# Gated levels on quarters of the array, four level slots, and the output gate moved to the output stage

## The chip, the cores and the metric

One core of a Trainium2 chip runs the kernel. A core has five engines that run their own instruction queues in order: TensorE (PE, matrix products; its weight loads are listed as PEld), VectorE (DVE), ScalarE (ACT), GpSimd (POOL) and SyncE (SP, which here issues all DMA transfers). They wait for each other by semaphores. Operands lie in SBUF, which has 128 partitions; matrix products end in PSUM. The metric is the device time of one execution in microseconds.

## What is computed

One layer for 2048 latent tokens of 1024 channels, with 256 context tokens ahead of them: normalisation and modulation, a projection to the inputs of two mixers, gated linear attention (GLA) and the gated delta rule (GDN), each run over the tokens in both directions with 4 heads, and an output part that normalises, gates and mixes both. What the change touches is the attention inside a chunk of GLA and the gates of the output:

```
def gla_chunked(q, k, v, g, s0):
...
        diff = bi[:, :, :, None, :] - bi[:, :, None, :, :]
        dec = jnp.exp(jnp.where(causal[:, :, None], diff, -jnp.inf))
        att = jnp.einsum('bhtd,bhsd,bhtsd->bhts', qi, ki, dec)
        o = jnp.einsum('bhtd,bhde->bhte', qi * jnp.exp(bi), s) + jnp.einsum('bhts,bhse->bhte', att, vi)
...
    ya = rmsnorm(oa, gla_onorm).reshape(b, t, GLA_V) * jax.nn.silu(ag)
    yb = rmsnorm(ob, gdn_onorm).reshape(b, t, GDN_V) * jax.nn.silu(bg)
    merged = gates[..., :D_MODEL] * jnp.matmul(ya, w_gla_out) + gates[..., D_MODEL:] * jnp.matmul(yb, w_gdn_out)
    return jnp.matmul(merged, w_o)
```

The decay in `att` is one number per pair of tokens and channel, so `att` isn't one matrix product of q and k. The kernel builds it from levels.

## The kernel before

The program has three stages: projections and the preparation of GDN (to about 1367 us of the profile), the recurrences (`phase_mix`, to about 1785 us), and the output (`phase_out`). A planner of the framework puts each engine's instructions in an order by its own costs, from generators that `weave` interleaves; the order on each engine is fixed when the program is built.

`phase_mix` takes 17 steps `si`. Step `si` works on two chunks of 128 tokens at once, chunk 2 + si forwards and the mirrored one backwards, for GLA in `gla_step` and, one step behind, for GDN in two `gdn_scan`. From step 8 on both directions of a chunk are there, and each step gets four `finish` generators, two for GLA (mi = 0, tile `og`) and two for GDN (mi = 1, tile `oi`).

**Levels.** `att` of the forward chunk (tile `at`, 128 keys by 128 queries by 4 heads, both directions in one tile since one fills the upper and one the lower triangle) is built for the levels m = 64, 32, 16, 8, 4, 2: at level m the pairs of tokens in the same block of 2m but different halves. For each level `gla_group` makes decayed keys `E` (L1117 on PE sums the logs of the decays, L1205 and L1208 on ACT take exponentials, L1215 on POOL multiplies by k) and decayed queries `ql` (L1214 on DVE), two levels to a group; `gla_lev` multiplies them (L1250) into one of two slots of the PSUM tile `lv` and copies what belongs to the level into `at`: for m = 64 two plain copies of a corner each on ACT (L1258), for the others a copy on DVE under a mask of all 128 columns (L1261). The levels 64 and 32 follow the step's outputs (`gla_out`, L1332 and L1337: attention times v, and q times the state `Sa`), the levels 16 and 8 and then 4 and 2 come alone later. What is next to each other in time is added by `gla_near` (L1238, L1240), and POOL starts `at` with the diagonal (L1268).

**GDN.** L1047 and L1058 multiply the state `Sb` with keys and queries, L1050, L1069, L1071 (`vn`), L1079, L1083 and L1089 go on to the new state and the output.

**Outputs.** `finish` loads the gate into a tile `fg` (4 buffers, L1388), sums the squares of the output (L1392 on ACT, four for each tile), scales it (L1395, POOL), transposes it (L1399, PE), multiplies it by gain and gate (L1400, DVE, in place in `fg`) and stores it to `d_y` (L1402). There are 32 of them, A to D in the prediction being the four of one step, in the order og, oi, oi, og. In the output stage `out_y` loads two halves of `d_y` of a block of 256 tokens (L1553, into the ring `wr` of 4 buffers) and splits each into a high and a low part (L131 on ACT, L134 on POOL), which `out_merge` (L1578) multiplies with the weights of both mixers; L1647 is the product with `w_o`. The blocks follow each other as 3, 4, 2, 5, 1, 6, 0, 7.

All transfers go out on SP in order, on 8 semaphores in turn, so that at most 8 are under way.

Of the kernel before, what the change touches and what calls it, by code (L numbers as in the profile page):

```python
# [22 lines left out]
P = 128  # L23
# [61 lines left out]
def const_i32():  # L85
    s = np.arange(P)[:, None]
    out = np.zeros((P, 2, len(MASK_LEVELS), 64), np.int32)
    for d in range(2):
        for i, m in enumerate(MASK_LEVELS):
            t = later_cols(d, m)[None, :]  # L90
            out[:, d, i, :] = ((s // (2 * m)) == (t // (2 * m))) & ((s // m) != (t // m))
    t = s.T
    pairs = [((s // (2 * m)) == (t // (2 * m))) & ((s // m) != (t // m)) for m in LEVELS[1:]]
    return np.concatenate([out.reshape(P, -1), *[x.astype(np.int32) for x in pairs]], 1)


class Build:
# [1044 lines left out]

    def slot(self):
        self.nslot += 1
        return self.lv[:, :, self.nslot % 2]

    @staticmethod
    def byhalf(ap):
# [40 lines left out]
                self.gla_kt(x[0])  # L1189

    def gla_group(self, r, i0):
        nc, q, k, at = self.nc, r["q"], r["k"], r["at"]
        E = self.gE.tile([P, 2, 2, 2, P], F32, name="E", bufs=3)
        ql = self.gq.tile([P, 2, 2, P], F32, name="ql", bufs=3)
        cols = (2 * P + i0 * P, 4 * P + i0 * P)
        for ct in range(2):
            ps = self.pe()
            v = ps.rearrange("p (l b n) -> p l b n", l=2, b=4)
            self.gla_sums(v[:, :, 1:3], r, 0, ct, cols)
            self.gla_sums(v[:, :, 0:4:3], r, 1, ct, cols)  # L1200
            for li in range(2):
                m = LEVELS[i0 + li]
                s = ps[:, 256 * li:256 * li + 256]
                if m == 64:
                    nc.scalar.activation(E[:, ct, li].rearrange("p x t -> p (x t)"), s, AF.Exp, scale=1.0 / 16)  # L1205
                    continue
                for x in range(2):
                    nc.scalar.activation(E[:, ct, li, x].rearrange("p (j e i) -> p e j i", e=2, i=m),  # L1208
                                         s[:, x * P:(x + 1) * P].rearrange("p (e j i) -> p e j i", e=2, i=m),
                                         AF.Exp, scale=1.0 / 16)  # L1210
            if ct == 0:
                yield
        for li in range(2):
            nc.vector.tensor_tensor(ql[:, li], E[:, :, li, 0], q, op=ALU.mult)  # L1214
            nc.gpsimd.tensor_tensor(E[:, :, li, 1], E[:, :, li, 1], k, op=ALU.mult)  # L1215
        yield
        return [(at, [E[:, ct, li, 1] for ct in range(2)], ql[:, li], LEVELS[i0 + li]) for li in range(2)]

    def gla_ones(self, r):
        nc, k, q = self.nc, r["k"], r["q"]  # L1220
# [11 lines left out]
        return w  # L1232

    def gla_near(self, r):
        nc, at, w = self.nc, r["at"], r["near"]
        pd = self.pe()
        for ct in range(2):
            nc.tensor.matmul(pd[:, 2 * ct:2 * ct + 2], w[:, ct], self.bones, start=True, stop=True)  # L1238
        B = [P, 4, P]
        nc.vector.copy_predicated(at, self.am[:, len(LEVELS) - 2].unsqueeze(1).broadcast_to(B),  # L1240
                                  pd[:, 0:4].unsqueeze(2).broadcast_to(B))

    def gla_lev(self, levs, behind=None):
        nc, got = self.nc, []
        for at, ks, ql, m in levs:
            ps = self.slot()
            for ct in range(2):
                for hp in range(2):
                    rows = slice(64 * hp, 64 * hp + 64)
                    mm = nc.tensor.matmul(ps[:, hp, ct], ks[ct][rows], ql[rows, ct], start=True, stop=True)  # L1250
                    self.behind(mm, behind)
                    self.last_lev = mm
            got.append((self.byhalf(at), ps, m))
        for at, ps, m in got:
            if m == 64:
                for x in range(2):
                    rows, cols = slice(64 * x, 64 * x + 64), slice(64 - 64 * x, 128 - 64 * x)
                    nc.scalar.copy(at[rows, :, :, cols], ps[rows, :, :, cols])  # L1258
            else:
                i = LEVELS.index(m) - 1  # L1260
                nc.vector.copy_predicated(at, self.am[:, i].unsqueeze(1).unsqueeze(1).broadcast_to([P, 2, 2, P]), ps)  # L1261

    def gla_step(self, f, b, prev):
        nc = self.nc
        self.gla_split(f)
        self.gla_split(b)
        at = f["at"] = f["kp"].tile([P, 4, P], F32, name="at", bufs=1)
        nc.gpsimd.tensor_tensor(at, self.diag[:, f["c"] - NCTX, :].unsqueeze(2).broadcast_to([P, 4, P]),  # L1268
                                self.ident.unsqueeze(1).broadcast_to([P, 4, P]), op=ALU.mult)
        yield  # L1270
        self.gla_ends(f)
        yield
# [10 lines left out]
        yield  # L1283
        if prev is not None:
            out, done = self.gla_out(prev, S)
        self.gla_lev(levs, out if prev is not None else None)
        if prev is not None:
            done()
            yield
            yield from self.gla_put(prev)  # L1290
        yield
        last = yield from self.gla_group(f, 4)
        yield
        self.gla_lev(more)
        yield
        self.gla_kt(b)
        f["near"] = self.gla_ones(f)
# [29 lines left out]
    def gla_out(self, pair, S):  # L1327
# [4 lines left out]
            nc.tensor.matmul(po[h % 2][:, 0, h // 2], f["at"][:, h], f["v"][:, h * P:(h + 1) * P],  # L1332
                             start=h < 2, stop=False, skip_group_check=True)
        for d, r in enumerate(pair):
            for h in range(4):
                ct, rows = h // 2, slice(64 * (h % 2), 64 * (h % 2) + 64)
                mm = nc.tensor.matmul(po[h % 2][:, d, ct], r["qe"][rows, ct], S[d][rows, ct], start=False,  # L1337
                                      stop=d == 1 and h >= 2, skip_group_check=True)

        def done():  # L1340
            o = self.og = f["prev"] if f["prev"] is not None else self.op.tile([P, 2, 4, P], F32, name="og")
# [41 lines left out]
    def finish(self, mi, l, src):  # L1383
        nc, wk = self.nc, self.wk
        if "o" in self.dbg:
            nc.sync.dma_start(self.dbg["o"][mi, l], self.flat(src))
        y = wk.tile([P, 4, P], F32, name="fg", bufs=4)
        nc.sync.dma_start(y, self.d_gate[l // 2, :, 4 * mi:4 * mi + 4, (l % 2) * P:(l % 2) * P + P])  # L1388
        sq = wk.tile([P, P], BF16, name="fsq", bufs=1)
        ss = wk.tile([P, 4], F32, name="fss", bufs=4)  # L1390
        for h in range(4):
# [5 lines left out]
        pt = self.pe()  # L1397
        for h in range(4):
            self.behind(nc.tensor.transpose(pt[:, h * P:(h + 1) * P], src[:, h], self.ident), mm)  # L1399
        nc.vector.scalar_tensor_tensor(self.flat(y), pt, self.pc[:, 64 + mi:65 + mi], self.flat(y),  # L1400
                                       op0=ALU.mult, op1=ALU.mult)
# [20 lines left out]
    def phase_mix(self):  # L1422
# [17 lines left out]
        self.am = mp.tile([P, len(LEVELS) - 1, P], I32, name="am")  # L1440
# [5 lines left out]
        self.lv = self.pool("ppg", 1, PSUM, ctx=gctx).tile([P, 2, 2, 2, P], F32, name="lv")  # L1446
# [109 lines left out]
    def out_y(self, b):  # L1556
# [2 lines left out]
        yl = yp.tile([P, 8, 256], F32R, name="yl")  # L1559
        for hf in range(2):  # L1560
            ks = slice(4 * hf, 4 * hf + 4)
            self.split(yh[:, ks], yl[:, ks], self.yraw.pop(0) if self.yraw else self.y_raw(b, hf))
        self.y2 = (yh, yl)

    def out_merge(self, b):
# [128 lines left out]
```

## Time and profile before

| | us |
|---|---|
| median of 3 runs | 2175.05 (2174.11 to 2176.63) |
| the profiled execution | 2176.2 |
| its span on the core | 2174.4 |
| PE busy in the span | 2089.3 (96%) |
| DVE, ACT, POOL busy | 1237.0, 888.1, 867.7 |

The span reaches from the first to the last instruction that the profiler saw; the execution's time has 1.8 us around it. The mean granted clock of TensorE was 0.988 of its full speed. A busy time is the union of an engine's instructions, and those of PE overlap: the time of a run of matmuls is better read from one start to the next. In a timeline, instructions of one kind that follow each other are one row with their count.

### The profile page before, as it was taken

Reading aid. Unit: us, or ns where it says so; the run is one execution under the profiler, and the core shown is the slowest. Engines: PE = TensorE matmul, PEld = TensorE weight load, DVE = VectorE, ACT = ScalarE, POOL = GpSimd, SP = SyncE. Lnnn points to the kernel's source line nnn. Section 1 sums busy time; section 2 is a strip of 40 time slices with the busy share of each in tenths; the row PEclk is TensorE's granted clock in tenths of the full one; section 3 lists DMA queues with packets and bytes.
Section 4 is the critical chain, followed back from the end, with each engine's and each line's share of the span. In section 5 each row is a group of like instructions: output and inputs, shape, how many; then the busy total and the mean of one; then the engine's idle time right before and its main releaser. Section 6 shows DMA issues by size and latency. Waiting matters only on the chain.

```text
span 2174.4 us, 39781 instructions
## 1 busy us (share of the span) xinstructions
PE 2089.3 (96%) x15072; PEld 1753.6 (81%) x15072; DVE 1237.0 (57%) x2183; ACT 888.1 (41%) x2180; POOL 867.7 (40%) x779
## 2 busy tenths in 40 slices
PE   5999999999999999999999999899989988999998
PEld 2688888888888888777777777788888887999888
DVE  3813555556777554555555555566678876344333
ACT  3644255554552223343444443344455554112111
POOL 2410122222231015665666662556566655222331
PEclk9999999999999999999999999999999989999999
DMA  7323122222222224344444443878779958443322
GB/s 279 110 85 115 50 68 64 67 62 66 61 65 81 74 84 138 118 146 146 141 147 151 129 139 114 300 279 307 262 262 312 299 177 265 131 127 116 102 85 81
DMA packets 275004, 315.67 MB, mean 145 GB/s; under 512 B 22280, under 2 KB 206716, under 8 KB 274812
## 3 DMA queue, kind: packets, MB, share of 16 engines
q1 hardware_dynamic: 274812, 313.12, 44.5%
q8 instruction: 119, 1.95, 0.4%
q14 instruction: 73, 0.60, 0.1%
HBM read 203.20 MB, written 109.84 MB: 144 GB/s over the span
## 4 chain that ended last, share of the span: by engine, by line
PE 83%; DVE 5%; ACT 4%; DMA 4%; issue 2%; SPq 1%; POOL 1%; DVEq 0%; POOLq 0%; ACTq 0%
PE pz L370 46%; PE pz L1647 8%; PE pm L1578 7%; PE pe L1117 2%; PE pz L1079 1%; PE pe L935 1%; PE pl L987 1%; PE pl L994 1%; PE lv L1250 1%; PE pl L995 1%; DMA g<-dg 1%; PE pz L1058 1%; DVE ql L1214 1%; PE pq L613 1%; ACT E L1208 1%
## 5 line engine op out<-in xcount | busy, mean ns | idle before, releaser
L370 PE MATMUL pz<-hi,wh 128*128 128x512 f32 (+1 forms) x1560 | 621.7, 399 | 1.6 <-DVE hi L133 1.6
L370 PE MATMUL pz<-lo,wh 128*128 128x512 f32 (+1 forms) x1560 | 600.6, 385 | 1.8 <-POOL lo L134 1.8
L370 PE MATMUL pz<-hi,wl 128*128 128x512 f32 (+1 forms) x1520 | 588.6, 387 | 0.0
L370 PEld LDWEIGHTS pz<-lo,wh 128*128 128x128 f32 x1560 | 294.8, 189 | 51.3 <-POOL lo L134 3.7
L370 PEld LDWEIGHTS pz<-hi,wh 128*128 128x128 f32 x1560 | 294.4, 189 | 48.0 <-DVE hi L133 2.5
L370 PEld LDWEIGHTS pz<-hi,wl 128*128 128x128 f32 x1520 | 286.3, 188 | 53.8 <-issue 0.4
L134 POOL TENSOR_TENSOR wl<-w,wh 128x1024 fp32r<-128x1024 f32 x44 | 108.8, 2475 | 437.3 <-ACT wh L131 311.9
L568 DVE SCALAR_TENSOR_TENSOR acc<-zpad,cw,acc 128x1024 f32<-128x1024 f32 x192 | 271.4, 1414 | 6.7
L1578 PE MATMUL pm<-yh,wab 128*128 128x256 f32 x1024 | 190.5, 287 | 0.9 <-ACT wab L131 0.9
L872 DVE CAST_PREDICATED U<-kit,pl 128x256 f16<-128x256 int32 x216 | 91.2, 431 | 139.4 <-PE pl L995 135.6
L1578 PEld LDWEIGHTS pm<-yh,wab 128*128 128x128 f32 x1024 | 163.5, 195 | 1.8 <-ACT wab L131 1.0
L1647 PE MATMUL pz<-wo,mh 128*128 128x512 f32 (+1 forms) x528 | 160.6, 387 | 0.0
L1578 PE MATMUL pm<-yl,wab 128*128 128x256 f32 x512 | 146.9, 287 | 0.2 <-POOL yl L134 0.2
L988 ACT CAST ppb<-pl 128x256 f16<-128x256 f32 x216 | 73.6, 374 | 167.6 <-PE pl L987 161.2
L1215 POOL TENSOR_TENSOR E<-E,ak 128x256 f32<-128x256 f32 x96 | 80.9, 863 | 101.8 <-ACT E L1205 51.6
L1647 PEld LDWEIGHTS pz<-wo,mh 128*128 128x128 f32 x528 | 98.2, 189 | 20.0
L134 DVE TENSOR_TENSOR sql<-sq,sqh 128x512 fp32r<-128x512 f32 (+1 forms) x36 | 28.0, 804 | 142.0 <-ACT sqh L131 141.8
L623 POOL TENSOR_TENSOR acc<-acc,sq 128x512 f32<-128x512 f32 x32 | 51.1, 1605 | 138.4 <-ACT sq L622 90.6
L1647 PE MATMUL pz<-wo,ml 128*128 128x512 f32 (+1 forms) x264 | 101.5, 385 | 0.0
L1578 PEld LDWEIGHTS pm<-yl,wab 128*128 128x128 f32 x512 | 100.2, 196 | 0.7 <-POOL yl L134 0.4
L134 POOL TENSOR_TENSOR yl<-wr,yh 128x1024 fp32r<-128x1024 f32 x16 | 40.2, 2529 | 135.7 <-ACT yh L131 135.7
L1652 DVE TENSOR_TENSOR mt<-pz,gtb 128x512 f32<-128x512 f32 (+1 forms) x33 | 22.3, 675 | 117.0 <-PE pz L1647 114.8
(297 smaller groups left out, 4182.9 us busy)
## 6 DMA issues: line engine op xcount, KB each, us to landing
dgate<-ob SPq DMA_DIRECT2D x96, 256.0 KB
gd<-dgd SPq DMA_DIRECT2D x32, 768.0 KB
w<-in_w_in SPq DMA_DIRECT2D x44, 512.0 KB
qk<-dqkv SPq DMA_DIRECT2D x32, 512.0 KB
ga<-dgate SPq DMA_DIRECT2D x64, 256.0 KB
dqkv<-acc SPq DMA_DIRECT2D x192, 64.0 KB
dgd<-tm SPq DMA_DIRECT2D x36, 256.0 KB
dgd<-n SPq DMA_DIRECT2D x36, 256.0 KB
```

Of the source, the lines that this page charges most:

```text
L134: getattr(nc, lo).tensor_tensor(dst_lo, src, dst_hi.bitcast(F32), op=ALU.subtract)
L370: nc.tensor.matmul(ps[:, 0:n], a[:, kk, :], b[:, kk, :], start=(k == 0), stop=(k == last - 1))
L568: nc.vector.scalar_tensor_tensor(acc, src, wcol, acc, op0=ALU.mult, op1=ALU.add)
L613: nc.tensor.matmul(u[4][:, 0:u[2]], self.ones, u[3][i], start=(i == 0), stop=(i == 1))
L623: nc.gpsimd.tensor_tensor(v, v, r, op=ALU.mult)
L872: self.nc.vector.copy_predicated(out, mv, data)
L988: nc.scalar.copy(ppl, pc.rearrange("p h (j i) -> p h j i", i=m))
L1117: self.nc.tensor.matmul(out, g[:, i, ct * P:(ct + 1) * P], self.wt[:, d, cols[0]:cols[1]], start=(j == 0), stop=(j == 1))
L1215: nc.gpsimd.tensor_tensor(E[:, :, li, 1], E[:, :, li, 1], k, op=ALU.mult)
L1578: nc.tensor.matmul(ps[:, half * 256:half * 256 + 256], wab[wi][:, k, j * P:(j + 1) * P], yy[:, k, :], start=(i == 0), stop=(i == 11))
L1647: nc.tensor.matmul(ps, aa[:, k, i * P:(i + 1) * P], wo[k][wi][:, cs], start=(j == 0), stop=(j == 23))
L1652: nc.vector.tensor_tensor(sq, ps, gtb[:, cs], op=ALU.mult)
```

## The change

Four things are changed.

- A level is multiplied by quarters: 64 keys by 64 queries for one head at a time (tiles of 64 rows and 64 columns of the array, L1257), only where the level has pairs: the diagonal blocks of 64 for m < 64, the other two for m = 64. Its slot in `lv` is 64 columns wide instead of 128, and there are four in the same PSUM. Masks, the copies under a mask, and the diagonal's product go by a tile `own` of the diagonal blocks; two ACT copies at the end (L1245) put it into `at`. The state's part of the output (L1337, now L1347) goes by quarters too, with 64 queries in place of 128.
- The levels 64, 32, 16 and 8 are multiplied together behind `gla_out`; only 4 and 2 stand alone.
- `finish` has no gate for 28 of 32 tiles (all but those of block 3): ACT (mi = 0, L1420) or DVE (mi = 1, L1418) multiplies by the gain on the way out of PSUM, and `fg` has two buffers.
- `out_y` loads the gates of 7 of the 8 blocks in two transfers of 512 KB and multiplies (L1589, DVE, 128 x 1024) before the split.

```diff
     def slot(self):
         self.nslot += 1
-        return self.lv[:, :, self.nslot % 2]
+        return self.lv[:, :, self.nslot % 4]
...
     def gla_near(self, r):
...
-        B = [P, 4, P]
-        nc.vector.copy_predicated(at, self.am[:, len(LEVELS) - 2].unsqueeze(1).broadcast_to(B),
+        B = [P, 4, 64]
+        nc.vector.copy_predicated(own, self.am[:, len(LEVELS) - 2].unsqueeze(1).broadcast_to(B),
                                   pd[:, 0:4].unsqueeze(2).broadcast_to(B))
+        for x in range(2):
+            half = slice(64 * x, 64 * x + 64)
+            nc.scalar.copy(at[half, :, half], own[half])
 
     def gla_lev(self, levs, behind=None):
         nc, got = self.nc, []
-        for at, ks, ql, m in levs:
+        for r, ks, ql, m in levs:
             ps = self.slot()
             for ct in range(2):
-                for hp in range(2):
-                    rows = slice(64 * hp, 64 * hp + 64)
-                    mm = nc.tensor.matmul(ps[:, hp, ct], ks[ct][rows], ql[rows, ct], start=True, stop=True)
-                    self.behind(mm, behind)
-                    self.last_lev = mm
-            got.append((self.byhalf(at), ps, m))
-        for at, ps, m in got:
+                for x in range(2):
+                    y = x if m < 64 else 1 - x
+                    keys, qs = slice(64 * x, 64 * x + 64), slice(64 * y, 64 * y + 64)
+                    for hp in range(2):
+                        rows = slice(64 * hp, 64 * hp + 64)
+                        mm = nc.tensor.matmul(ps[keys, hp, ct], ks[ct][rows, keys], ql[rows, ct, qs], start=True, stop=True)
+                        self.behind(mm, behind)
+                        self.last_lev = mm
+            got.append((r, ps, m))
+        for r, ps, m in got:
             if m == 64:
                 for x in range(2):
                     rows, cols = slice(64 * x, 64 * x + 64), slice(64 - 64 * x, 128 - 64 * x)
-                    nc.scalar.copy(at[rows, :, :, cols], ps[rows, :, :, cols])
+                    nc.scalar.copy(self.byhalf(r["at"])[rows, :, :, cols], ps[rows])
             else:
                 i = LEVELS.index(m) - 1
-                nc.vector.copy_predicated(at, self.am[:, i].unsqueeze(1).unsqueeze(1).broadcast_to([P, 2, 2, P]), ps)
+                nc.vector.copy_predicated(self.byhalf(r["own"]),
+                                          self.am[:, i].unsqueeze(1).unsqueeze(1).broadcast_to([P, 2, 2, 64]), ps)
...
-        self.gla_lev(levs, out if prev is not None else None)
+        self.gla_lev(levs + more, out if prev is not None else None)
...
         last = yield from self.gla_group(f, 4)
         yield
-        self.gla_lev(more)
-        yield
...
         for d, r in enumerate(pair):
-            for h in range(4):
-                ct, rows = h // 2, slice(64 * (h % 2), 64 * (h % 2) + 64)
-                mm = nc.tensor.matmul(po[h % 2][:, d, ct], r["qe"][rows, ct], S[d][rows, ct], start=False,
-                                      stop=d == 1 and h >= 2, skip_group_check=True)
+            for ct in range(2):
+                for x in range(2):
+                    half = slice(64 * x, 64 * x + 64)
+                    for hp in range(2):
+                        rows = slice(64 * hp, 64 * hp + 64)
+                        mm = nc.tensor.matmul(po[hp][half, d, ct], r["qe"][rows, ct, half], S[d][rows, ct], start=False,
+                                              stop=d == 1 and ct == 1, skip_group_check=True)
...
-        y = wk.tile([P, 4, P], F32, name="fg", bufs=4)
-        nc.sync.dma_start(y, self.d_gate[l // 2, :, 4 * mi:4 * mi + 4, (l % 2) * P:(l % 2) * P + P])
+        gated = l // 2 == self.blocks[0]
+        if gated:
+            y = wk.tile([P, 4, P], F32, name="fg", bufs=2)
+            nc.sync.dma_start(y, self.d_gate[l // 2, :, 4 * mi:4 * mi + 4, (l % 2) * P:(l % 2) * P + P])
...
+        else:
+            y = wk.tile([P, 4, P], F32, name="fg", bufs=2)
+            if mi:
+                nc.vector.tensor_scalar(self.flat(y), pt, gain, None, op0=ALU.mult)
+            else:
+                nc.scalar.mul(self.flat(y), pt, gain)
...
-            self.split(yh[:, ks], yl[:, ks], self.yraw.pop(0) if self.yraw else self.y_raw(b, hf))
+            y = self.yraw.pop(0) if self.yraw else self.y_raw(b, hf)
+            if b != self.blocks[0]:
+                g = self.rp.tile([P, 8, P], F32, name="wr").rearrange("p (a b) c -> p a (b c)", b=2)
+                nc.sync.dma_start(g, self.d_gate[b][:, ks])
+                nc.vector.tensor_tensor(y, y, g, op=ALU.mult)
+            self.split(yh[:, ks], yl[:, ks], y)
```

What moves is seen best at three places. The first is TensorE's queue in a step of the first half, from the state's part of the output (L1337 before, L1347 after) to the last pair of levels. Before:

```order
L1337 MATMUL pz<-Sa_15950,q_15876 128x128 x4
L1250 MATMUL lv<-ql,E 128x128 [waits Pool_49]
L1250 MATMUL lv<-ql,E 128x128 x3
L1250 MATMUL lv<-ql,E 128x128 [waits Pool_49]
L1250 MATMUL lv<-ql,E 128x128 x3
...
L1226 MATMUL pe<-kf,g_16171 128x128 [waits DMAHW7_49,PE_49,Activation_49]
L1250 MATMUL lv<-ql,E 128x128 [waits DVE_49,Pool_49]
L1250 MATMUL lv<-ql,E 128x128 x3
...
L1047 MATMUL pz<-Sb_16343,qk 128x128 x3
L1250 MATMUL lv<-ql,E 128x128 [waits DVE_49,Pool_49]
L1250 MATMUL lv<-ql,E 128x128
```

After:

```order
L1347 MATMUL pz<-Sa_16048,q_15968 64x128 x8
L1347 MATMUL pz<-Sa_16051,q_15974 64x128 x8
L1257 MATMUL lv<-ql,E 64x64 [waits Pool_49]
L1257 MATMUL lv<-ql,E 64x64 x7
L1257 MATMUL lv<-ql,E 64x64 [waits Pool_49]
L1257 MATMUL lv<-ql,E 64x64 x7
L1257 MATMUL lv<-ql,E 64x64 [waits Pool_49]
L1257 MATMUL lv<-ql,E 64x64 x3
L1257 MATMUL lv<-ql,E 64x64 [waits Activation_49]
...
L1048 MATMUL pz<-Sb_16471,qk 128x128 x3
L1257 MATMUL lv<-ql,E 64x64 [waits DVE_49,Pool_49]
L1257 MATMUL lv<-ql,E 64x64 x3
```

Before, the three pairs of levels stand at three places, the last one behind all eight L1047. After, four levels stand behind L1347, and the last pair stands behind the first four L1048 and ahead of the other four.

The second place is ScalarE's queue in a step of the second half, around the copies of level 64 (L1258 before, L1265 after). E with 2x16x4 and 2x32x2 are the exponentials of the levels 4 and 2, `fsq` the squared sums of `finish`. Before:

```order
L1137 COPY akt<-pe 128x256 [waits PE_49]
L1208 ACTIVATE E<-pe 128x2x16x4 [waits DVE_49,PE_49]
L1208 ACTIVATE E<-pe 128x2x16x4
L1208 ACTIVATE E<-pe 128x2x32x2 x2
L1392 ACTIVATE fsq,fss<-og 128x128 [waits DMAHW0_49,DVE_49,Pool_49]
L1392 ACTIVATE fsq,fss<-og 128x128 [waits DVE_49,Activation_49]
L1392 ACTIVATE fsq,fss<-og 128x128 [waits Activation_49]
L1258 COPY at<-lv 64x2x2x64 [waits PE_49]
L1258 COPY at<-lv 64x2x2x64
L1208 ACTIVATE E<-pe 128x2x16x4 [waits PE_49]
L1208 ACTIVATE E<-pe 128x2x16x4
L1208 ACTIVATE E<-pe 128x2x32x2 x2
```

After:

```order
L1138 COPY akt<-pe 128x256 [waits PE_49]
L1404 ACTIVATE fsq,fss<-og 128x128 [waits DMAHW4_49,DVE_49,Pool_49]
L1404 ACTIVATE fsq,fss<-og 128x128 [waits DVE_49,Activation_49]
L1404 ACTIVATE fsq,fss<-og 128x128 [waits Activation_49] x2
L1265 COPY at<-lv 64x2x2x64 [waits PE_49]
L1265 COPY at<-lv 64x2x2x64
L1209 ACTIVATE E<-pe 128x2x16x4 [waits PE_49]
L1209 ACTIVATE E<-pe 128x2x16x4
L1209 ACTIVATE E<-pe 128x2x32x2 x2
L1209 ACTIVATE E<-pe 128x2x16x4 [waits PE_49]
L1209 ACTIVATE E<-pe 128x2x16x4
L1209 ACTIVATE E<-pe 128x2x32x2 x2
```

Four of the eight exponentials were ahead of the squared sums and the copies; all eight are now behind them, and the squared sums ahead of the copies are four instead of three.

The third is ScalarE's queue at the exponentials of the levels 64 and 32 of the next chunk (L1205 and L1208 before, L1206 and L1209 after), where the fourth output of the step is finished. Before:

```order
L1393 ACTIVATE fss<-fss,cb 128x4 [waits Activation_49]
L1394 ACTIVATE fss<-fss 128x4 [waits Activation_49]
L1205 ACTIVATE E<-pe 128x256 [waits PE_49]
L1208 ACTIVATE E<-pe 128x2x2x32 x2
L1205 ACTIVATE E<-pe 128x256 [waits PE_49]
L1208 ACTIVATE E<-pe 128x2x2x32 x2
L131 CAST gh_19593<-g_19567 128x256 [waits DMAHW1_49,PE_49]
L1126 ACTIVATE E_18962<-pe 128x512 [waits PE_49,Pool_49]
```

After:

```order
L1405 ACTIVATE fss<-fss,cb 128x4 [waits Activation_49]
L1406 ACTIVATE fss<-fss 128x4 [waits Activation_49]
L1206 ACTIVATE E<-pe 128x256 [waits PE_49]
L1209 ACTIVATE E<-pe 128x2x2x32 x2
L1420 ACTIVATE fg<-pe,pc 128x512 [waits DMAHW2_49,DMAHW5_49,DMAHW1_49,DVE_49]
L1206 ACTIVATE E<-pe 128x256 [waits PE_49]
L1209 ACTIVATE E<-pe 128x2x2x32 x2
L1127 ACTIVATE E_19370<-pe 128x512 [waits PE_49,Pool_49]
L1209 ACTIVATE E<-pe 128x2x4x16 [waits PE_49]
```

The product with the gain, L1420, now stands between the two halves of these exponentials. It waits on three DMA semaphores; one of them is that of the store that empties its buffer.

## Rows read from the trace of the kernel before

**Rows 1.** Windows: stretch, its us, busy us and instructions of each engine, PE clock, DMA share, GB/s.

```profile
1391.00:1604.00 213.00, 197.32 (x1937) 180.25 (x1936) 144.83 (x301) 99.16 (x382) 123.37 (x144) 0.99 0.83 289
1604.00:1760.00 156.00, 142.53 (x1376) 132.06 (x1377) 129.55 (x278) 91.51 (x448) 104.41 (x118) 1.00 0.88 285
...
1828.00:2174.00 346.00, 339.10 (x2139) 307.65 (x2137) 140.33 (x229) 62.01 (x139) 95.28 (x93) 0.99 0.36 118
```

**Rows 2.** Chain that ended last, first half: start us, us, what.

```profile
1484.75 2.05 PE pz L1079 x16
...
1507.53 2.05 PE pz L1079 x16
...
1513.15 7.88 DMA do<-oi
1521.09 6.10 DMA g<-dg
...
1596.35 6.13 DMA g<-dg
```

**Rows 3.** PE timeline, first half: start us, us to the last end, instructions, count.

```profile
1490.98 1.16 PE L1337 MATMUL pz<-Sa,q 64*128 64x128 f32 x16
1491.97 1.06 PE L1250 MATMUL lv<-ql,E 64*128 64x128 f32 x16
1492.96 0.39 PE L1117 MATMUL pe<-wt,gh 128*128 128x256 f32 x1
...
1495.01 1.16 PE L1250 MATMUL lv<-ql,E 64*128 64x128 f32 x16
...
1496.48 1.73 PE L1047 MATMUL pz<-Sb,qk 128*128 128x128 f32 x14
...
1499.25 0.39 PE L1117 MATMUL pe<-wt,gh 128*128 128x256 f32 x1
```

**Rows 4.** PE timeline, two windows, 1423.02 to 1423.06 and 1423.0 to 1424.2.

```profile
1423.03 0.42 PE L645 MATMUL pz<-gw,sc 128*32 128x256 f32 x4
...
1423.03 1.50 PE L645 MATMUL pz<-gw,sc 128*32 128x256 f32 x24
```

**Rows 5.** ACT timeline, first half.

```profile
1493.90 1.48 ACT L1208 ACTIVATE E<-pe 128x128 f32<-128x128 f32 x8
```

**Rows 6.** POOL timeline, first half.

```profile
1495.10 1.67 POOL L1215 TENSOR_TENSOR E<-E,ak 128x256 f32<-128x256 f32 x2 [1.68 <-ACT E L1208]
```

**Rows 7.** PE timeline, second half; in brackets the idle time ahead and its releaser.

```profile
1645.13 1.16 PE L1250 MATMUL lv<-ql,E 64*128 64x128 f32 x16 [1.12 <-DVE at L1261]
...
1661.78 1.16 PE L1337 MATMUL pz<-Sa,q 64*128 64x128 f32 x16
...
1666.78 1.16 PE L1250 MATMUL lv<-ql,E 64*128 64x128 f32 x16 [1.19 <-DVE at L1261]
...
1671.32 1.09 PE L1313 MATMUL pz<-av,akt 128*64 128x128 f32 x16
```

**Rows 8.** ACT timeline, second half.

```profile
1653.73 0.39 ACT L1205 ACTIVATE E<-pe 128x256 f32<-128x256 f32 x1 [0.83 <-PE pe L1117]
...
1665.85 0.80 ACT L1208 ACTIVATE E<-pe 128x128 f32<-128x128 f32 x4
...
1679.25 0.39 ACT L1205 ACTIVATE E<-pe 128x256 f32<-128x256 f32 x1 [0.83 <-PE pe L1117]
```

**Rows 9.** SP timeline: DMA issues, second half.

```profile
1650.18 1.03 SPq L1402 DMA_DIRECT2D dy<-fg  x2
...
1653.83 1.56 SPq L1388 DMA_DIRECT2D fg<-dgate  x2
...
1675.53 1.03 SPq L1402 DMA_DIRECT2D dy<-fg  x2
...
1681.31 4.27 SPq L1388 DMA_DIRECT2D fg<-dgate  x4
```

**Rows 10.** Groups of instructions, output stage: busy us, mean ns, idle before and releaser.

```profile
L134 DVE TENSOR_TENSOR wo<-wr,wo 128x1024 fp32r<-128x1024 f32 x2 | 2.4, 1222 | 3.4 <-ACT wo L131 3.4
```

More of the change, by code (lines that the diff above doesn't have):

```diff
@@ L93, in const_i32 @@
     pairs = [((s // (2 * m)) == (t // (2 * m))) & ((s // m) != (t // m)) for m in LEVELS[1:]]
-    return np.concatenate([out.reshape(P, -1), *[x.astype(np.int32) for x in pairs]], 1)
+    own = [np.where(s < 64, x[:, 0:64], x[:, 64:128]) for x in pairs]
+    return np.concatenate([out.reshape(P, -1), *[x.astype(np.int32) for x in own]], 1)
 class Build:
@@ L1191, in gla_group @@
     def gla_group(self, r, i0):
[L1192 removed]
+        nc, q, k = self.nc, r["q"], r["k"]
         E = self.gE.tile([P, 2, 2, 2, P], F32, name="E", bufs=3)
@@ L1216, in gla_group @@
         yield
-        return [(at, [E[:, ct, li, 1] for ct in range(2)], ql[:, li], LEVELS[i0 + li]) for li in range(2)]
+        return [(r, [E[:, ct, li, 1] for ct in range(2)], ql[:, li], LEVELS[i0 + li]) for li in range(2)]
     def gla_ones(self, r):
@@ L1234, in gla_near @@
     def gla_near(self, r):
-        nc, at, w = self.nc, r["at"], r["near"]
+        nc, at, own, w = self.nc, r["at"], r["own"], r["near"]
         pd = self.pe()
@@ L1266, in gla_step @@
         self.gla_split(b)
-        at = f["at"] = f["kp"].tile([P, 4, P], F32, name="at", bufs=1)
-        nc.gpsimd.tensor_tensor(at, self.diag[:, f["c"] - NCTX, :].unsqueeze(2).broadcast_to([P, 4, P]),
-                                self.ident.unsqueeze(1).broadcast_to([P, 4, P]), op=ALU.mult)
+        f["at"] = f["kp"].tile([P, 4, P], F32, name="at", bufs=1)
+        own = f["own"] = f["kp"].tile([P, 4, 64], F32, name="own", bufs=1)
+        nc.gpsimd.tensor_tensor(own, self.diag[:, f["c"] - NCTX, :].unsqueeze(2).broadcast_to([P, 4, 64]),
+                                self.id64.unsqueeze(1).broadcast_to([P, 4, 64]), op=ALU.mult)
         yield
@@ L1399, in finish @@
             self.behind(nc.tensor.transpose(pt[:, h * P:(h + 1) * P], src[:, h], self.ident), mm)
-        nc.vector.scalar_tensor_tensor(self.flat(y), pt, self.pc[:, 64 + mi:65 + mi], self.flat(y),
-                                       op0=ALU.mult, op1=ALU.mult)
+        gain = self.pc[:, 64 + mi:65 + mi]
+        if gated:
+            nc.vector.scalar_tensor_tensor(self.flat(y), pt, gain, self.flat(y), op0=ALU.mult, op1=ALU.mult)
+        else:
[4 more added lines that the diff above has]
+                nc.scalar.mul(self.flat(y), pt, gain)
         nc.sync.dma_start(self.d_y[l // 2, :, mi * 4:mi * 4 + 4, (l % 2) * P:(l % 2) * P + P], y)
@@ L1439, in phase_mix @@
             nc.vector.memset(self.bones[64 * x:64 * x + 64, 1 - x:2 - x], 0.0)
-        self.am = mp.tile([P, len(LEVELS) - 1, P], I32, name="am")
+        self.am = mp.tile([P, len(LEVELS) - 1, 64], I32, name="am")
+        self.id64 = mp.tile([P, 64], F32, name="id64")
+        for x in range(2):
+            half = slice(64 * x, 64 * x + 64)
+            nc.vector.tensor_copy(self.id64[half], self.ident[half, half])
         wt = mp.tile([P, 2, WL], F32R, name="wt")
@@ L1445, in phase_mix @@
         self.ppe = self.pool("ppe", 3, PSUM, ctx=ctx)
-        self.lv = self.pool("ppg", 1, PSUM, ctx=gctx).tile([P, 2, 2, 2, P], F32, name="lv")
+        self.lv = self.pool("ppg", 1, PSUM, ctx=gctx).tile([P, 2, 4, 2, 64], F32, name="lv")
         self.nslot, self.last_lev = 0, None
```

## The prediction

> **What bounds the kernel now.** I read the table of windows first. The projections before 1391 us aren't touched by the diff. The recurrent stage falls into two halves: in steps 0 to 7 (1391 to 1604 us) TensorE is busy 197.3 of 213 us, in steps 8 to 15 (1604 to 1760 us), where outputs are finished too, 142.5 of 156; the DMA engines are busy 83% and 88% [rows 1]. The output stage is TensorE's almost alone, 339.1 of 346 us, with DMA at 36% and DVE at 140 us [rows 1]. So there is something to win only in the two halves.
>
> The chain of waits shows what a step is. From one start of L1079 to the next an undisturbed step takes 22.8 us (1484.75 to 1507.53); the next one takes 26.3, because a store of 7.88 us and a load of 6.10 us end last in it [rows 2]. A third such piece stands at 1596.35. Where a transfer ends last, faster matmuls buy nothing. So two or three of the first eight steps gain little, and I count 0.7 of what TensorE saves there.
>
> **Levels: half the columns, four quadrants.** (Line numbers are those before; only L1420 and L1589, which are new, are those after.) Before, one level is 8 matmul instructions (4 in the code, each issued as two) on half the array's rows, 128 columns wide. Two levels take 0.99 us (1490.98 to 1491.97 is L1337, 1491.97 to 1492.96 a pair of levels) [rows 3]. After, a level is 16 instructions on a quarter of the array, 64 columns wide. If four run at a time, a pair takes half, 0.5 us; if still only two do, 32 instructions of half the width take 0.99 as before. No quadrant matmul is in the trace. The nearest row is L645, four column tiles: its four matmuls start within the 0.04 us of one window, and 24 of them take 1.50 us, 62 ns each where one alone is 256 columns wide [rows 4]. That is four at a time with nothing visible between starts, so I take 0.5 us and keep 0.99 as the other end. Six levels a step would be 1.5 us.
>
> The Trainium skill, "TensorEngine Tiling (Array Packing)", section Instruction Overhead, says against this that a matmul has about 60 cycles of its own and that a tiling factor should not be taken from a dimension that is already small. By that rule the 64 columns would gain little and the sum below would lose its gain in the first half. Rows 4 show four narrow tiles overlapping, but at 256 columns, so no run here shows it at 64.
>
> **But the last pair then waits for its operands.** The order moves four levels together behind L1337, which takes away one stand-alone group, and brings the last pair (4, 2) forward. Before, first half: L1337 starts at 1490.98 and the matmul behind the last pair at 1499.25, 8.27 us [rows 3]. After, counted from 1490.98: L1337 0.99, four levels 1.0 and some 0.1 for going in and out of the tiling, the work that now stands between 1492.96 and 1495.01 2.05, the L1226 behind the stand-alone group 0.4 (1495.01 to 1496.48 less the group's 1.1), six of the fourteen L1047 at 0.12, 0.7: the last pair is reached at 1496.2. Its keys come from ScalarE (eight exponentials, 1493.90 and 1.48 us long) [rows 5] and then GpSimd (two products, 1495.10 to 1496.77) [rows 6]; nothing in the change makes these earlier. So the second level of the pair starts at 1496.85, ends at 1497.1, the other eight L1047 (0.96) end at 1498.1: **1.15 us a step** instead of the 1.6 that 1.5 us of matmuls and one stand-alone group's cost would give. Eight steps at 0.7: **-6.5 us** (bounds 0 and -13).
>
> Second half: L1337 starts at 1661.78, L1313 behind the last pair at 1671.32; in between TensorE idles 1.19 us for a predicated copy [rows 7]. With four slots that wait goes. But on ScalarE all eight exponentials of the last pair now stand behind four squared sums and the two copies of level 64, where before four of them had been done ahead: the row of four at 1665.85 [rows 8] becomes eight, and one more squared sum (about 0.4, my estimate) stands ahead. They end near 1667.75, the products near 1669.05 (the 1.67 of rows 6, begun after six of eight), the pair at 1669.35, then six L1047 and the eight short matmuls that stood ahead of the pair before, 1.6: 1671.0, which saves 0.35. In the step before, a second wait of 1.12 stands in this place [rows 7]; it goes as well, so there it is 1.45. I take 0.85 in each of 7 steps: **-6 us** (bounds -2.5 and -19).
>
> **Output tiles: two buffers instead of four.** A step finishes four outputs, A to D. C needs A's buffer back, D needs B's, and a buffer is back when its store has landed. Before, each buffer was filled by a gate load that waited for just this landing, so the rows show it: stores issued at 1650.18, first gate load at 1653.83; 1675.53 and 1681.31 [rows 9]. That is 3.65 and 5.8 us, alternating over six steps. C is on DVE, right ahead of the second L1071, whose result TensorE reads only in the second half of L1079, and A's store is out before B's: its wait is no longer than D's and lies beside it. D is on ScalarE between the two exponentials L1205 of the next pair, and behind it stand L1126, all of L1208 and the weights' splits, for which TensorE waits. ScalarE's idle there is 0.83 us, spent on TensorE [rows 8], so nothing covers it. B's evacuation is first on DVE after the change, so its store goes out when A's did. With 0.6 us for D (a ScalarE pass of this size, estimated from 0.39 for half the columns), the second L1205 moves from 1653.73 to 1654.5 and from 1679.25 to 1682.0 [rows 8, 9]: 0.8 and 2.75 us. Less load on the queues should shorten the long ones, so I take 1.3 in each of 7 steps: **+9 us** (bounds 0, if the stores land in time, and +20).
>
> **Gate loads leave the stage.** 28 loads of 256 KB, about 1 MB of the 7.4 MB that a step of the second half moves (285 GB/s by 26 us) [rows 1]. They also held SP: the one at 1681.31 waited for a store, and every load behind it on that queue waited too [rows 9]. Loads that end on the chain come earlier: **-5 us** (0, if those are bound by the DMA engines, to -12).
>
> **At no cost,** with what hides it. DVE's shorter predicated copies, GpSimd's smaller initial product, the two added ScalarE copies (0.4 each) and A's product on ScalarE: DVE is busy 129.6 of 156 us, ScalarE 91.5, GpSimd 104.4, and the copies stand in gaps [rows 1]; were they uncovered, 0.8 us a step. L1337, 32 instructions of 128 columns in quadrants for 16 on halves: 0.99 four at a time; two at a time it doubles, +13 us over 15 steps. In the output stage 14 products of 1024 columns, by the split of that size 1.22 us each [rows 10], 17 us on a DVE that idles 200 us there, and 7.3 MB on queues at 36%; uncovered 17 us. At the passage to that stage two products stand ahead of the last weight splits, some 10 us before TensorE needs them.
>
> **Sum.** -6.5 - 6 + 9 - 5 = -8.5. The profiled execution took 2176.2 us (span 2174.4 and 1.8 around it), 1.15 above the median of the runs: 2167.7 by it, **2167** beside the median of 2175.05.
>
> **Rivals.** (1) *The store's wait decides, slower.* Mechanism: D on ScalarE, at 2.75 us in every step and not in every second one. 7 x 2.75 = 19 for 9: 2177; with the loads' -5 at 0, 2182. It turns the sign where D's wait passes about 2.5 us a step. For it: no slack on ScalarE [rows 8]. Against: half the stores land in 3.65 us [rows 9]. (2) *Quadrants run two at a time.* The first half's -6.5 shrinks to -1, the second half loses 2.5: 2175, no change; if L1337 suffers likewise, 2185 and more. For it: no such tile is in the trace. Against: rows 4. (3) *The stores land in time and the loads were the second half's bound.* D's wait 2 us in all, loads -9, second half -9: 2176.2 - 6.5 - 9 + 2 - 9 = 2153.7, 2153 beside the median. For it: SP held by the gate loads [rows 9], 88% DMA [rows 1].
>
> **How the numbers follow.** A measurement of this kernel tells 0.2%, 4.35 us, from no change: faster is below 2170.7, slower above 2179.4. The sum as taken (2159 to 2176 by the middles of its bounds): 0.48. Rival 3 (2147 to 2158): 0.22. Rival 2: 0.14. Rival 1: 0.16. Faster: 0.33 of the sum and all of rival 3, 0.55. Same: 0.15, most of rival 2 (0.09) and a little of rival 1 (0.03), 0.27. Slower: the rest of the two, 0.18. For 8 in 10 the range runs from 2151 (a third of rival 3 is below) to 2181 (half of rivals 1 and the doubled L1337 above).
>
> **What the profile after would show.** Right: the four levels take 1.0 us for 64 instructions; from the start of L1337 to the matmul behind the last pair there are 7.1 us in the first half; the last pair waits for GpSimd's product; ScalarE's second product (L1420) waits for a store in every step from 8 on; the products of the output stage (L1589) aren't on the chain; DMA share below 0.8 between steps 8 and 15. Wrong: a pair of levels near 0.99 us; L1337 at 2 us; L1420 without a wait; or undisturbed steps of the first half that stay at 22.6 us, which would mean that the recurrence through ScalarE and DVE, not TensorE, sets them.

## The result and the profile after

The changed kernel takes 2163.64 us (median of 4 runs, 2161.77 to 2166.79), the kernel before 2175.84 on the same chip: ratio 0.9948, 95% interval 0.9933 to 0.9962, so 8 to 15 us faster. Forecast were 2167 us and a range of 2151 to 2181. The time and its sign were right; of the terms of the sum three were not, and they cancelled, so it is in part luck that the forecast came within 4 us.

Its windows, cut where the halves of the recurrent stage end (columns as in [rows 1]: PE, PEld, DVE, ACT, POOL, then granted clock, DMA share and GB/s), and the second half before, cut at the same place:

```profile
1391.00:1597.00 206.00, 188.39 (x2489) 173.21 (x2487) 138.34 (x306) 107.39 (x403) 122.03 (x147) 0.99 0.85 296
1597.00:1752.00 155.00, 136.43 (x1753) 124.57 (x1752) 111.47 (x266) 99.66 (x463) 101.39 (x117) 1.00 0.80 258
...
1820.00:2165.00 345.00, 333.32 (x2108) 302.67 (x2106) 157.58 (x236) 60.69 (x137) 87.65 (x92) 0.99 0.40 133
```

```profile
1608.00:1764.00 156.00, 142.53 (x1378) 132.06 (x1377) 129.02 (x277) 91.13 (x445) 102.53 (x116) 1.00 0.89 286
```

The first half ends at 1597 and not near 1608, the second is as long as before at a DMA share of 0.80 for 0.89, the output stage runs at the same 45 us a block. To compare kernels I take four points from TensorE's timeline of each profiled execution: the start of the state's part of the output in steps 8 and 14, the start of the second block's product with `w_o`, and the end.

| profiled execution | 1391 to step 8 | step 8 to 14 | step 14 to block 2 | rest | span |
|---|---|---|---|---|---|
| before | 217.6 | 155.7 | 109.9 | 300.1 | 2174.4 |
| after | 206.0 | 155.1 | 112.7 | 300.2 | 2165.0 |

So 11.6 us come from the first eight steps, 0.6 from the next six, and 2.8 go back in the passage to the output. The profiled execution after is the slowest of its four: the spans differ by 9.4 us, the medians by 12.2, and no profile shows where the other 3 us lie.

TensorE's timeline in a step of the first half (columns as in [rows 3]) is the place of the prediction's walk:

```profile
1484.46 1.10 PE L1347 MATMUL pz<-Sa,q 64*64 64x128 f32 x32
1485.39 1.11 PE L1257 MATMUL lv<-ql,E 64*64 64x64 f32 x64
1486.43 0.39 PE L1118 MATMUL pe<-wt,gh 128*128 128x256 f32 x1
...
1489.46 0.46 PE L1257 MATMUL lv<-ql,E 64*64 64x64 f32 x16
1490.28 0.46 PE L1257 MATMUL lv<-ql,E 64*64 64x64 f32 x16 [0.36 <-POOL E L1216]
...
1491.59 0.36 PE L1118 MATMUL pe<-wt,gh 128*128 128x256 f32 x1
```

The four levels, 64 instructions, take 1.04 us (1485.39 to 1486.43), 16 ns from start to start: so four quarters run at a time; before, 0.99 us went to two levels alone [rows 3]. From L1347 to the matmul behind the last pair there are 7.13 us; 7.1 were forecast. The last pair waits 0.36 us for GpSimd's product, as the walk had it. L1347 with twice the instructions takes 0.93 us, no longer than before.

The waits of the changed kernel, first half and second half (total us, times, longest):

```profile
PE pz L1339 <- DVE oi L1091: 6.7, 8, 2.5
...
PE pz L1080 <- DVE vn L1072: 5.7, 8, 0.9
...
PE lv L1257 <- POOL E L1216: 2.5, 7, 0.4
...
PE pe L1227 <- ACT E L1209: 7.7, 7, 1.5
...
PE pe L1411 <- POOL oi L1407: 4.6, 5, 1.2
...
PE lv L1257 <- POOL E L1216: 3.4, 11, 0.4
...
ACT fg L1420 <- DMA dy<-fg: 1.6, 2, 0.8
DVE fg L1418 <- DMA dy<-fg: 1.5, 2, 1.0
```

The same two waits before, first half:

```profile
PE pz L1079 <- DVE vn L1071: 4.3, 7, 1.2
PE pz L1332 <- DVE oi L1090: 3.6, 8, 0.6
```

Grown in the first half are the waits of TensorE for `oi` and `vn`, the recurrence of GDN through DVE, from 7.9 to 12.4 us: an undisturbed step fell only from 22.6 or 22.8 to some 22 us, not by the 1.15 of the walk. In the second half the waits for level slots (some 1.1 us in each step before [rows 7]) are gone, and others stand in their place: TensorE waits for the exponentials of the levels 4 and 2 (7.7 us, at the transposes L1227, which need a buffer that they free), for the scaled outputs (4.6) and for GpSimd's products (3.4). The waits for stores that the profile names come to 3.1 us.

Of the prediction's signs, the 1.04 us, the 7.13 us and the wait for GpSimd's product came as forecast; the DMA share is 0.80, at its border, and the undisturbed steps lie between the two sides. Two did not come: ScalarE's product L1420 waits for a store in two steps alone, and L1589 stands on the chain, for 0.09 us, in the passage to the output (shown below).

### The profile page after: what moved, and what is told of

It reads as the page before. It is cut to its first block, busy times and chain, and to the rows that moved or that the text cites. A ratio compares the mean times of both kernels' runs of the same rounds, so it can differ in the third digit from the quotient of the medians.

```text
span 2165.0 us, 41811 instructions
## 1 busy us (share of the span) xinstructions
PE 2067.1 (95%) x16096; PEld 1731.8 (80%) x16096; DVE 1227.0 (57%) x2185; ACT 906.5 (42%) x2226; POOL 858.6 (40%) x779
## 5 line engine op out<-in xcount | busy, mean ns | idle before, releaser
L554 ACT COPY zpad<-pz 128x512 f32<-128x512 f32 x48 | 28.2, 587 | 137.5 <-PE pz L371 137.5
```

Source lines behind the costliest of these rows:

```text
L554: nc.scalar.copy(zpad[:, 1 + r0:1 + r0 + nr, 1:1 + GW], ps[:, 0:n].rearrange("p (r w) -> p r w", w=GW))
```

## The experiments

All ratios are to the kernel before on the same chip, with 95% intervals; a microsecond is 0.046%. Line numbers are those of each kernel.

**The levels alone.** `finish` and `out_y` as before, all else as changed.

> The changed kernel with the gates back in the recurrent stage (gate loads, four buffers, product in front of the store) and no product in the output stage. Theory A, the levels give the gain in the first half and the gate move gives nothing net: the first half (to the start of the eighth step's state part) is 10 to 12 us shorter, the second half 0 to 3, the passage to the output unchanged; 2161 to 2166. Rival B, the gate loads' leaving gives it (the eighth step alone gained 3.2 us, and gates are loaded there): 2169 or more.

Measured: 0.9933 (0.9914 to 0.9952), 2162.5 us. The levels alone give 14.6 us, as much as the whole change or more; rival B falls. Theory A has the time but not the parts: in the profiled execution, the slowest with 2171.2 us, the halves take 203.4 and 170.4 us and the passage 104.5, so 14 less, 15 more and 5 less than before. Where the median gains its 14.6 us beyond the first half is thus not shown. The long second half ran at a lower granted clock,

```profile
1391.00:1594.00 203.00, 186.76 (x2487) 171.36 (x2486) 136.66 (x306) 107.03 (x401) 122.38 (x147) 1.00 0.84 296
1594.00:1764.00 170.00, 146.32 (x1757) 135.81 (x1756) 121.19 (x276) 95.46 (x459) 101.20 (x116) 0.91 0.85 276
```

0.91 where the kernel before has 1.00. "The levels" are quarters, four slots and the new order in one; no run takes these apart.

**The gate move alone,** on the kernel before.

> The kernel before with the gate move alone (two buffers, gates in the output stage), levels as before. Theory A: first half unchanged but for its last step, second half 0 to 4 us shorter by the loads, passage to the output 2 to 3 longer: 2172 to 2177. Rival B: the first half's last step and the second half together 8 to 10 us shorter: 2166 to 2170.

Measured: 1.0034 (1.0022 to 1.0046), 2183.2 us. Both missed: it is slower by 7.4 us. Its second half takes 163.0 us, and its waits there show why:

```profile
DVE fg L1408 <- DMA dy<-fg: 6.8, 3, 2.9
ACT fg L1410 <- DMA dy<-fg: 6.5, 4, 1.9
...
PE pe L1117 <- DVE fg L1408: 3.3, 3, 1.2
...
PE pe L1117 <- ACT fg L1410: 1.3, 1, 1.3
PE pe L1117 <- DVE fg L1404: 1.2, 2, 0.6
```

The stores that the prediction feared: 13.3 us of waits for them, as much on DVE as on ScalarE, and TensorE then waits for the two engines' products, mostly for DVE's (L1404 is the product of the block that is still gated, and no store's).

**Four buffers for the outputs,** in the changed kernel.

```diff
-        y = wk.tile([P, 4, P], F32, name="fg", bufs=2)
+        y = wk.tile([P, 4, P], F32, name="fg", bufs=4)
```

> The changed kernel with four output buffers again, nothing else. The prediction's store wait (9 us): 2153 to 2157. Theory A, in which the trace's waits for a store (1.6 us on ScalarE, 1.5 on DVE) are all that it costs: 2161 to 2164.

Measured: 0.9930 (0.9912 to 0.9948), 2160.5 us. Half a microsecond below theory A's range, and far from the 9 us: the two buffers cost about 4 us here by the ratios, and as the two intervals overlap, it may be nothing.

**Two blocks gated in the recurrent stage,** in the changed kernel.

```diff
-        gated = l // 2 == self.blocks[0]
+        gated = l // 2 in self.blocks[:2]
...
-            if b != self.blocks[0]:
+            if b not in self.blocks[:2]:
```

> The changed kernel with the first two output blocks gated in the recurrent stage instead of the first alone, so that no gate load and product of the output stage falls into the passage to it. Theory A, the passage lost 2.7 us by these: 2160 to 2162. Rival, the passage lost it by something else (the order of the weight splits, later stores): 2163 to 2165.

Measured: 0.9941 (0.9922 to 0.9960), 2162.7 us. Between the two, and not told from the changed kernel. The passage is 110.7 us for 112.7 in the profiles. In the changed kernel's chain a gate load of 4.88 us ends last ahead of the second block:

```profile
1839.04 4.88 DMA wr<-dgate
...
1844.04 0.09 DVE wr L1589
```

With the block gated earlier, a gate load of the next block stands in the same place of the chain:

```profile
1835.41 3.67 DMA wr<-dgate
```

So the edit did not free the passage of gate loads, and whether they are what it lost stays open.

**The gate move alone with four buffers.** The diff of the second experiment with `bufs=4`.

> The kernel before with the gate move alone, but with four output buffers as before. The gate move with two buffers cost 7.4 us, and its trace has 13 us of waits for stores on DVE and ScalarE. Theory A, these waits are the cost, as the prediction put it for this place: 2172 to 2177 (the 9 of the prediction off). Rival, the cost is the products and gate loads in the output stage or the passage: 2181 to 2184.

Measured: 0.9972 (0.9962 to 0.9983), 2168.2 us. Against two buffers 13.5 us: the ring's price in the order of before, clear of noise, and without it the gate move gives 6.1 us (4 to 8), more than theory A had; the rival falls.

**The gate loads left out,** in the kernel before (no gate is applied).

> The kernel before without the gate loads of the recurrent stage and without the gate itself (the gate is not applied; four buffers). The prediction's 5 us for the loads: 2169 to 2172. Rival, the second half doesn't wait for the volume of these loads: 2174 to 2177.

Measured: 0.9987 (0.9975 to 1.0000), 2172.8 us: 2.8 us, between the two, with an interval that ends at no change. In its profile the second half, where the prediction had the loads' gain, is not shorter at all (157.9 us for 155.7). How much of the gate move's 6 us is the loads' leaving therefore stays open.

**The decays of the last pair early,** in the changed kernel.

```diff
         self.gla_qe(b)
         yield
+        last = yield from self.gla_group(f, 4)
+        yield
         if prev is not None:
             out, done = self.gla_out(prev, S)
...
         yield
-        last = yield from self.gla_group(f, 4)
-        yield
         self.gla_kt(b)
```

> The changed kernel with the decays of the levels 4 and 2 (their sums, exponentials and products) in front of the step's output instead of behind it. Theory A, the second half is held by these exponentials behind four squared sums on ScalarE (7.7 us of L1227 waiting for ScalarE, 3.4 of the pair waiting for GpSimd): second half 6 to 10 us shorter, and the first half's stall of 0.4 a step gone: 2152 to 2158. Rival, the recurrence of the state through ScalarE and DVE sets the steps: 2161 to 2165.

> The same with four output buffers and the first two output blocks gated in the recurrent stage. If the three edits add up (3 for the buffers, 1 for the block, by the medians so far): 3 to 5 us less than with the early decays alone. If each only uncovers the next wait: the same as that one within 2 us.

Measured: 1.0007 (0.9995 to 1.0020), 2175.5 us, and with four buffers and two blocks 0.9927 (0.9907 to 0.9948), 2158.4 us. Neither theory of the first run holds, nor either of the second: four buffers and two blocks give 17 us on top of the early decays, not 3 to 5 or none. The first half does get shorter (200.1 and 199.8 us), but the second takes 173.7 and 163.7. Of the kernel with four buffers, from the second half: TensorE's timeline, ScalarE's copies of level 64, DVE's first copy under a mask behind them, and windows of 4 us:

```profile
1649.30 0.28 PE L1118 MATMUL pe<-wt,gl 128*128 128x256 f32 x1
1652.36 0.69 PE L1257 MATMUL lv<-ql,E 64*64 64x64 f32 x32 [2.78 <-DVE own L1268]
```

```profile
1649.62 0.73 ACT L1265 COPY at<-lv 64x256 f32<-64x256 f32 x2
```

```profile
1650.38 0.45 DVE L1268 COPY_PREDICATED own<-am,lv 128x256 f32<-128x256 int32 x1 [3.22 <-ACT at L1265]
```

```profile
1644.00:1648.00 4.00, 4.00 (x116) 3.81 (x115) 2.87 (x5) 3.81 (x21) 3.18 (x4) 1.00 0.93 319
1648.00:1652.00 4.00, 1.58 (x15) 1.38 (x13) 1.41 (x5) 3.90 (x21) 1.31 (x2) 1.00 0.91 303
1652.00:1656.00 4.00, 3.61 (x54) 3.25 (x54) 3.28 (x12) 2.67 (x10) 3.83 (x5) 0.71 0.66 228
1656.00:1660.00 4.00, 4.00 (x21) 3.77 (x18) 1.87 (x5) 0.75 (x3) 1.84 (x2) 0.50 0.62 203
1660.00:1664.00 4.00, 4.00 (x34) 3.92 (x33) 2.82 (x9) 2.14 (x6) 0.00 (x0) 0.93 0.90 206
```

The planner now puts twelve squared sums of `finish` ahead of the two ScalarE copies of level 64. DVE idles 3.22 us until these are done and only then starts its copies under a mask; the fifth level waits 2.78 us for those. TensorE does little for some 3 us, and then its granted clock falls to 0.50, the lower of its two levels (1.2 GHz), in one window of 4 us, with 0.71 and 0.93 around it: 4 x (0.29 + 0.50 + 0.07) = 3.4 us of full clock are lost in this step beside the wait, by my estimate from these windows.

**The level-64 copies on DVE,** with the early decays, four buffers and two blocks; with the early decays alone; and alone in the changed kernel.

```diff
-                    nc.scalar.copy(self.byhalf(r["at"])[rows, :, :, cols], ps[rows])
+                    nc.vector.tensor_copy(self.byhalf(r["at"])[rows, :, :, cols], ps[rows])
```

> The last run (early decays, four buffers, two blocks gated) with the two copies of level 64 on DVE instead of ScalarE. Theory A: there they stood behind twelve squared sums, TensorE waited 2.8 us a step for a level slot, and its granted clock then fell to 0.5 for some 4 us; without that wait the clock stays at 1.0 in the second half, which is 10 to 16 us shorter: 2142 to 2149. Rival, the clock falls there for another reason, or DVE becomes the second half's bound: 2155 to 2160.

> The changed kernel with the early decays and the level-64 copies on DVE, two buffers, one block gated. Theory A (exponentials behind squared sums held the second half, and the two buffers cost 3 to 13 us once nothing else stands ahead of them): 5 to 14 us above the run with four buffers and two blocks, 2150 to 2158. Rival, two buffers are free here as in the changed kernel: within 4 us of it.

> The changed kernel with the level-64 copies on DVE alone, decays where the change has them. Theory A: the eight exponentials lose two copies of 0.37 ahead of them on ScalarE, still behind four squared sums: 0 to 6 us shorter, 2158 to 2164. Rival, it is these copies and not the place of the exponentials that held the second half: as much as with both edits, 2150 to 2156.

Measured: 0.9941 (0.9925 to 0.9958), 1.0016 (1.0003 to 1.0028) and 0.9946 (0.9930 to 0.9963); 2163.1, 2178.6 and 2162.9 us. The first two lie above both theories and both rivals, the third within its theory A. My edit for the wait failed. In the first of the three it is still there, 3.20 us in this step:

```profile
1661.35 0.69 PE L1257 MATMUL lv<-ql,E 64*64 64x64 f32 x32 [3.20 <-DVE own L1268]
```

The slot now waits for DVE, whose masked copies have L1231 between them, and that takes its operand from ScalarE behind the same squared sums. The second, against the first, shows the price of two buffers (and of one gated block) again, 16 us; the third that the copies were not what held the changed kernel's second half.

**Early decays in the first eight steps only,** with four buffers and two blocks.

```diff
+        early = f["c"] - NCTX < NLAT // 2
+        if early:
+            last = yield from self.gla_group(f, 4)
+            yield
...
+        if not early:
+            last = yield from self.gla_group(f, 4)
+            yield
```

> The changed kernel with four output buffers, two blocks gated in the recurrent stage, and the decays of the levels 4 and 2 early in the first eight steps alone (no squared sums on ScalarE there). If the halves add up as the profiles have them: first half 200 us as with the early decays everywhere, second half 153 as with four buffers and late decays, granted clock 1.0 in it: 2153 to 2157. If the first half's gain is given back later, or the second half was short only by chance: 2159 to 2162.

Measured: 0.9918 (0.9905 to 0.9932), 2158.7 us; above the forecast, below its rival. It beats both kernels, the changed one by 5 us by the medians and 6.5 by the ratios, with intervals from two comparisons that just don't overlap. From the changed kernel with four buffers alone (0.9930) it can't be told. Its halves in the profiled execution took 203.1 and 158.7 us, both at a granted clock of 0.97:

```profile
1391.00:1594.00 203.00, 187.46 (x2474) 175.12 (x2472) 130.73 (x303) 106.95 (x398) 120.42 (x144) 0.97 0.84 294
1594.00:1753.00 159.00, 136.88 (x1758) 127.88 (x1761) 117.17 (x269) 98.54 (x463) 101.91 (x117) 0.97 0.82 262
```

So the halves as other profiles had them didn't add up. The lower clock may have a part in it; no run shows how much.

## Why the prediction was right, step by step

**Levels in quarters: right.** Four at a time, 1.04 us for 64 instructions. The Trainium skill, "TensorEngine Tiling (Array Packing)", section Instruction Overhead, advises against taking a tiling factor from a dimension that is small already; at 64 columns this trace shows no loss of that kind, with four levels in 1.04 us where two took 0.99 at 128 columns. The prediction took the rows of the four column tiles instead [rows 4], and they held.

**The first half's 6.5 us: sign right, size wrong, 11.6 us.** The walk's 7.1 us was met. The step that failed is the discount, "I count 0.7 of what TensorE saves there", and with it the picture of one gain in every undisturbed step. Steps with a transfer at their end shortened as well, the 24.9, 25.9 and 26.0 us of before to 24.1, 24.1 and 24.0; the undisturbed ones shortened by less than 1.15, since `vn` and `oi` then end last, and one rose from 22.6 to 23.9. The eighth step, which the walk took for one like the others, gave most, 23.1 to 20.0 us; in the kernel before, TensorE waits there for exponentials:

```profile
1603.86 0.39 PE L1117 MATMUL pe<-wt,gh 128*128 128x256 f32 x1 [1.43 <-ACT E L1208]
```

In the profiles of the five kernels with quarters and late decays the first half takes 198.7 to 206.0 us, in the four with whole levels 212.6 to 217.6: on average 12.1 less, and some 3 of it in the eighth step. That a transfer's start is set by compute (the 7.88 us store of [rows 2] goes out when DVE has its data) would explain that these steps follow TensorE; I haven't tested it.

**The stores' wait: real, but not at its size in this kernel.** 9 us were forecast, and the ring of two costs 13.5 us in the order of before; with early decays it is 16 and 17, a second gated block's share in it. In the changed kernel itself it is about 4, and not clear of noise. Nor is ScalarE its one place: in the gate move alone DVE's product waits for stores up to 2.9 us where ScalarE's waits up to 1.9, though the prediction had DVE's wait as the shorter. ScalarE's product with the gain still waits there, but less, and TensorE hardly for it:

```profile
1671.27 0.69 ACT L1420 ACTIVATE fg<-pe,pc 128x512 f32<-128x512 f32 x1 [0.83 <-DMA dy<-fg]
```

That is 0.83 us in this step, where the gate move alone had waits up to 1.9. Why the rest is covered is argued, not shown: TensorE comes to this place later, after its waits for the exponentials.

**Gate loads' leaving: not shown.** 5 us were forecast; the gate move with four buffers gives 6.1, the loads alone 2.8 with no change just inside the interval, and none of it in the second half of that profile.

**The second half's level gain: not found.** 6 us were forecast, and in sum with stores and loads -2; the profiles have -0.6. The waits for slots went as forecast, but the walk's own point, eight exponentials behind four squared sums, weighed more than its 0.85 us a step allowed: TensorE's 7.7 us at L1227 are at the transposes ahead of the last pair, where I had looked only at the pair. The profiles have the second half (steps 8 to 14) of each combination:

| second half, us | whole levels | quarters |
|---|---|---|
| gates in the recurrent stage, four buffers | 155.7 | 170.4 (clock 0.91) |
| gates moved, four buffers | 152.9 | 152.9 |
| gates moved, two buffers | 163.0 | 155.1 |

Each is one execution. With the gates moved, the levels give nothing there with four buffers, and 8 us with two, as if they hid most of what the ring costs with whole levels. The parts measured alone, -14.6 for the levels and -6.1 for the gates with four buffers, make -20.7, both together give -15.2; the intervals of the three runs leave room for a plain sum. That ScalarE's queue holds the second half is what the waits suggest, argued and not shown; the runs that were to show it brought a wait of their own.

**At no cost: right but for the passage,** where 2.8 us were lost in the profiles, and 8.2 against the levels alone (104.5 us), from a cause that stays open. The product L1589 takes 1.22 us as estimated, and the output stage didn't grow.

Of the three rivals the first was at work without the levels (slower by 7.4 us), the second fell with the first row of quarters, and the third's short second half was not found: even with four buffers it is 2.8 us shorter than before (152.9 us), not 16.

## What to carry to other kernels

A ring that is cut from four buffers to two can turn a store's landing into a wait; its price depends on what else the engine in front of it waits for, about 4 us in one order and 13 to 17 in others, so it is to be measured in the order that will stay. A gain that is walked on one queue holds up to the next queue: put the squared sums, the exponentials and the slots on one time axis before moving work. Quarters of the array cost nothing here, where the product was blocked already: half the work took half the time.

## What was not expected of the hardware

In the second half TensorE is busy most of the time (146.3 of 170 us with the levels alone), and yet waits inside a step were followed by some microseconds at the lower clock level, as the windows above show. The length of one wait doesn't tell whether. With early decays and four buffers the same wait of 2.78 us, one step earlier, was not followed by a fall:

```profile
1627.27 0.69 PE L1257 MATMUL lv<-ql,E 64*64 64x64 f32 x32 [2.78 <-DVE own L1268]
```

```profile
1624.00:1628.00 4.00, 1.22 (x38) 0.98 (x37) 2.50 (x9) 3.84 (x20) 1.89 (x3) 1.00 0.88 334
1628.00:1632.00 4.00, 3.97 (x40) 3.58 (x41) 3.63 (x13) 2.44 (x7) 4.00 (x6) 1.00 0.55 171
```

With the levels alone it fell behind two shorter waits close together:

```profile
1685.21 0.69 PE L1257 MATMUL lv<-ql,E 64*64 64x64 f32 x32 [1.45 <-DVE own L1268]
...
1687.36 1.01 PE L1239 MATMUL pe<-bones,qk 128*128 128x2 f32 x4 [0.78 <-POOL qk L1232]
```

```profile
1684.00:1688.00 4.00, 2.01 (x39) 1.77 (x40) 4.00 (x11) 3.90 (x23) 3.77 (x6) 0.85 0.99 373
1688.00:1692.00 4.00, 4.00 (x26) 3.65 (x27) 2.71 (x10) 0.15 (x2) 1.67 (x2) 0.50 0.85 294
1692.00:1696.00 4.00, 2.76 (x18) 2.57 (x16) 2.52 (x6) 2.55 (x11) 1.91 (x2) 0.80 0.81 271
```

The kernel before, with a wait of some 1.1 us in each step [rows 7], kept 1.00 in its second half; the four kernels with early decays throughout had 0.88 to 0.90 there. So a wait may cost more than its length, and an edit that shortens TensorE's work but leaves waits in a step may lose by it. What decides whether the clock falls, these runs don't show.
